# One encoder layer on one core: the second LayerNorm's scale taken block by block, its parameter rows in a ring slot, and the late branch moved into the 11th pair of experts

## The chip, the core and the metric

The kernel runs on one core of one Trainium2 chip. The metric is the device time of one execution in microseconds (us). Before the change it is 1922.2 us, the median of three runs (1920.51 to 1925.04).

## The reference, cut to what matters

One layer of an encoder over 256 tokens of width 2048. A mixer (not shown) gives y, and then:

```python
x = _layer_norm(ALPHA * x + y, ln1_g, ln1_b)
y = _hmoe(x, ...)      # 32 experts, each token goes to 2 of them
x = _layer_norm(ALPHA * x + y, ln2_g, ln2_b)

def run(args):         # one expert on its tokens
    e, idx, w = args
    xb = xf[idx]
    h = jax.nn.silu(xb @ w1[e]) * (xb @ w3[e])
    return (h @ w2[e]) * w[:, None]

def _layer_norm(x, g, b):
    mu = xf.mean(-1, keepdims=True)
    var = jnp.mean(jnp.square(xf - mu), -1, keepdims=True)
    return (xf - mu) * lax.rsqrt(var + LN_EPS) * g + b
```

w1 and w3 (gate and up) are 2048 x 512 per expert, w2 (down) is 512 x 2048, all float32: 12 MB for one expert and 384 MB for the 32.

## The kernel before, in words

The first 990 us or so compute the mixer, the first LayerNorm and the router. The rest, with which the change deals, is the expert phase and the second LayerNorm (LN2).

**Pairs.** The 32 experts are worked in 16 pairs (`for p in range(NP)`). Each expert has 64 places for tokens, so a pair fills the 128 rows. A pair does `gate_up` (16 steps of 4 products, `gu`; the trace shows each float32 product as two records), then `dispatch` of the next pair's tokens (`ps_d`), `turn_hidden` and `turn_places` (`pt_hs`, `pt_oh`), `down` (`py`, 32 products), and `combine` (`ps_c`), which adds the weighted rows into `acc`, the layer's sum of two halves of 128 tokens by 2048. The two last combines of a pair are kept in `pending` and run beside the next pair's first steps. `gate_up` takes a table `beside`, which says what other work is put ahead of which step.

**Loads.** A pair reads 24 MB in 24 loads of 1 MB: 8 of the gate matrices, 8 of the up matrices, 8 of the down matrices. Those of the last pair's down matrices go by the column blocks `LAST`. SP issues all of them in the order of the program (`loads_in_order`, a schedule by hand). `places()` hands out the buffer of each load: 18 slots of 1 MB in five rings (`RINGS`, taken in the order of `TURN`), tiles named `er`. A load waits until the last reader of its slot is done. It also waits for the load eight before it, because there are eight completion semaphores (DMAHW0 to DMAHW7), so at most eight are in flight. Semaphores DMASW are those of loads that POOL (GpSimd) issues.

**LayerNorm rows.** `ln1_g`, `ln1_b` and `ln2_g` lie as rows of 512 in `lnrow`, a part of `wrf` that belongs to the kernel for good. `ln_row(r)` spreads a row over the 128 partitions by a product with a column of the identity (`ps_ln`). `residual()`, in the pair with index 3 (the 4th), adds ALPHA times LN1's output to `acc`: eight calls beside steps 4 to 11 of that pair, each beginning with one `ln_row`. `ln2_scale()`, in the last pair, spreads `ln2_g` into one ring slot (four `ln_row` and four ScalarE copies), and loads `ln2_b` into another by one broadcast load of 1 MB.

**The end.** `down_last` does the last pair's down products by the blocks `LAST`; the combine of each block also takes the statistics (`bn_stats`) of the sum. Then come `ln2_stats()`, the branch `tc.If(most > CAP)` and the application of LN2 to eight pieces of 128 by 512. The branch handles experts with more than 64 tokens (`late_block`). It is not taken for these inputs. Six pieces are done by two VectorE passes each (L1316, L1317), two by ScalarE and two GpSimd passes, and each piece is stored when it is done.

The functions that the diff touches:

Of the kernel before, what the change touches and what calls it, by code (L numbers as in the profile page):

```python
# [19 lines left out]
P = 128  # L20
# [29 lines left out]
def kernel(ctx: ExitStack, tc: tile.TileContext, a, out):  # L50
# [173 lines left out]
    wr = glob.tile([P, KT, 36], F32, name="wr")  # L224
# [518 lines left out]
    def places():  # L743


        turn = [i for i in TURN for i in [i[0]] * i[1]]
        index = (i for i in count() if i not in (18, 19, 20))
        slot = lambda i: rings[i].tile([P, 2048], F32, tag="er", name="er")
        for i in turn:
            yield next(index), slot(i)  # L750
        yield 18, ys_p[0].tile([P, 2048], F32, tag="ys", name="er_ys")
        for s in range(2):
            yield 19 + s, x1p[0].tile([P, D], F32, tag=f"x1{s}", name="er_x1")
        while True:
            for i in turn:
                yield next(index), slot(i)

    place = places()

    def prefetch():  # L760
        i, t = next(place)
# [248 lines left out]
    lnrow = wrf[0:16, 0:512]  # L1010
    for j, k in enumerate(("ln1_g", "ln1_b", "ln2_g", "ln2_b")):
        nc.gpsimd.dma_start(lnrow[4 * j:4 * j + 4], a[k].rearrange("(m c) -> m c", c=512))

    def ln_row(r):

        pg = sm("ps_ln")
        PE.matmul(pg, ident[:16, r:r + 1].to_broadcast([16, P]), lnrow, start=True, stop=True)
        return pg

    gb2 = [], []  # L1020
    b2 = a["ln2_b"].rearrange("(o c) -> o c", o=1)

    def ln2_scale():
        while len(loads) - 1 not in loaded:
            prefetch()
        for b in gb2:
            b.append(next(place)[1])
        nc.sync.dma_start(gb2[1][0], b2.to_broadcast([P, D]))
        for c in range(4):
            S.activation(gb2[0][0][:, 512 * c:512 * (c + 1)], ln_row(8 + c), AF.Copy)  # L1030
            yield

    def residual():

        for c in range(4):
            cc = slice(512 * c, 512 * (c + 1))
            pg = ln_row(c)
# [7 lines left out]
            pg = ln_row(4 + c)  # L1045
# [10 lines left out]
    def late_block(e, b):  # L1056
# [3 lines left out]
        oh = ex_p[0].tile([P, 2, CAP], F32, tag="oh", name="oh_l", bufs=2)  # L1060
        ow = ex_p[0].tile([P, 2, CAP], F32, tag="ow", name="ow_l")
# [12 lines left out]
        for wv, o0 in ((w1v, 0), (w3v, 512)):  # L1074
            for k0 in range(0, KT, 2):
                wt = rings[2].tile([P, 1024], F32, tag="er", name="er_l")
                nc.sync.dma_start(wt, wv[ds(e, 1), :, k0 * DE:(k0 + 2) * DE].rearrange("e p f -> (e p) f"))
# [3 lines left out]
        hst = hs_p[0].tile([P, 2, DE], F32, tag="hs", name="hs_l")  # L1081
# [14 lines left out]
        for hf in range(2):  # L1096
            py = acc2("py_l")
            for k in range(4):
                wt = rings[2].tile([P, 1024], F32, tag="er", name="er_l")
                nc.sync.dma_start(wt, w2v[ds(e, 1), :, k, hf * 1024:(hf + 1) * 1024].rearrange("e p c -> (e p) c"))  # L1100
# [86 lines left out]

    def combine(c, ys, cb, w=512, first=False, last=False):
# [5 lines left out]
        for s in range(2):  # L1194
# [5 lines left out]
            if last:  # L1200
                V.bn_stats(stat[:, s, LAST.index((c, w))], o)

# [39 lines left out]

    acc = ys = None
    for p in range(NP):
# [3 lines left out]
        beside = {1: [finish], 2: [finish]} if p else {i: [lambda k=k: dispatch_part(0, k) for k in ks]  # L1248
# [3 lines left out]
        if p == RESIDUAL:  # L1252
            res = residual()
            beside |= {i: [lambda: next(res)] for i in range(4, 12)}
        if last:
            scale2 = ln2_scale()
            beside |= {i: [lambda: next(scale2)] for i in (10, 12, 14, 15)}
        hst = gate_up(p, beside)
        if last:
            S.activation(glob.tile([P, 1], F32, tag="warm", name="warm2"), hst[:, 0, 0:1], AF.Sqrt, bias=epsc, scale=0.0)  # L1260
            hT = turn_hidden(hst)
            cb, ws = turn_places(p)
            down_last(hT, cb, ws)
# [15 lines left out]
    products_in_order.close()  # L1279
    lmv = ex_p[0].tile([P, 2, 2], F32, name="lmv")  # L1280
# [3 lines left out]
    def ln2_stats():  # L1284
        for s in range(2):
            V.bn_aggr(lmv[:, s], stat[:, s])
        S.activation(lrs, lmv[:, :, 1], AF.Sqrt, bias=epsc)
        V.reciprocal(lrs, lrs)
        V.scalar_tensor_tensor(lnb, lmv[:, :, 0], -1.0, lrs, op0=OP.mult, op1=OP.mult)

    ln2_stats()
    loads_in_order.close()
    with tc.If(most > CAP):
        with tc.For_i(0, NE) as e:
            n = nc.values_load(cnt[0:1, ds(e, 1)], min_val=0, max_val=T)
            for b in range(1, T // CAP):
                with tc.If(n > b * CAP):
                    late_block(e, b)
        for s in range(2):
            for i, (c, w) in enumerate(LAST):  # L1300
                V.bn_stats(stat[:, s, i], acc[s][:, c:c + w])
        ln2_stats()


    ctx.enter_context(tc.manual_schedule(engines={mybir.EngineType.DVE, mybir.EngineType.Pool, mybir.EngineType.SP}))
    for i, pooled in ((0, 0), (1, 1), (2, 0), (5, 1), (3, 0), (4, 0), (7, 0), (6, 0)):
        s, c = divmod(i, 4)
        cc = slice(512 * c, 512 * (c + 1))
        g2, bb2 = (t[0][:, cc] for t in gb2)
        o = acc[s][:, cc]  # L1310
        if pooled:
            S.activation(o, o, AF.Identity, bias=lnb[:, s:s + 1], scale=lrs[:, s:s + 1])
            G.tensor_tensor(o, o, g2, op=OP.mult)
            G.tensor_tensor(o, o, bb2, op=OP.add)
        else:
            V.scalar_tensor_tensor(o, o, lmv[:, s, 0:1], g2, op0=OP.subtract, op1=OP.mult)  # L1316
            V.scalar_tensor_tensor(o, o, lrs[:, s:s + 1], bb2, op0=OP.mult, op1=OP.add)  # L1317
# [38 lines left out]
```

## Time and profile before

| what | value |
|---|---|
| median of three runs | 1922.2 us (1920.51 to 1925.04) |
| the profiled execution's own time | 1924.37 us |
| its span, first to last instruction | 1922.7 us |
| mean granted TensorE clock | 0.994 of full speed |
| busy: PE, DVE, ACT, POOL | 97%, 42%, 30%, 4% of the span |
| moved by DMA | 576.59 MB, mean 300 GB/s |

The profiled execution is 1.67 us longer than its span, and 2.2 us above the median of the runs. Busy shares are means over a dense first half, in which PE computes with the weights split in two parts, and the expert phase; the two have different limits and are to be read apart. PE is TensorE, DVE VectorE, ACT ScalarE, POOL GpSimd, and SP the engine that issues the weight loads. A q behind an engine's name means its instruction queue.

### The profile page before, as it was taken

What the parts mean: (1) busy time and instruction counts of PE and PEld (TensorE: products, weight loads), DVE (VectorE), ACT (ScalarE), POOL (GpSimd) and SP (SyncE); (2) the same over time, 40 slices, a digit from 0 to 9 for tenths busy, and PEclk for the clock granted to TensorE, in tenths of its full rate; (3) what the DMA queues carried; (4) which work ended last, traced back from release to release, by engine and by line L of the source; (5) the groups of instructions that cost most, each with busy time, mean ns of one, the idle gap of its engine ahead of it and who ended that gap; (6) DMA issues with size and microseconds to landing.
All of it is one profiled execution on the core that took longest, in us unless ns stands there. A gap on an engine that the chain in (4) does not pass through costs nothing. (4 is left out here: it accounts for less than half of the span.)

```text
span 1922.7 us, 28567 instructions
## 1 busy us (share of the span) xinstructions
PE 1865.2 (97%) x12006; PEld 1318.5 (69%) x12007; DVE 803.0 (42%) x1257; ACT 575.5 (30%) x807; POOL 74.4 (4%) x95
## 2 busy tenths in 40 slices
PE   9999999999999999999999999999999999999995
PEld 8989999999999999997753444444344443443432
DVE  6477685476545555555521234122122121221215
ACT  5464444466444444443430111011011010110111
POOL 3100001021000000000000000000000000000001
PEclk9999999999999999999999999999999999999997
DMA  9554565644555555679499999999999999999995
GB/s 276 179 171 143 156 195 176 186 143 137 177 186 187 187 186 187 229 257 356 140 420 396 419 419 420 419 419 420 419 419 420 419 420 419 419 420 420 420 414 200
DMA packets 148806, 576.59 MB, mean 300 GB/s; under 512 B 12348, under 2 KB 14784, under 8 KB 100416
## 3 DMA queue, kind: packets, MB, share of 16 engines
q1 hardware_dynamic: 146896, 571.52, 78.7%
q0 software_dynamic: 1776, 3.18, 0.6%
q8 instruction: 96, 1.57, 0.3%
q14 instruction: 38, 0.31, 0.0%
HBM read 572.54 MB, written 2.10 MB: 299 GB/s over the span
## 5 line engine op out<-in xcount | busy, mean ns | idle before, releaser
L177 PE MATMUL ps_t<-xh,whi 128*128 128x256 f32 x1856 | 522.7, 282 | 0.8 <-ACT xh L110 0.8
L177 PE MATMUL ps_t<-xl,whi 128*128 128x256 f32 x1856 | 521.4, 281 | 0.2 <-DVE xl L111 0.2
L177 PE MATMUL ps_t<-xh,wlo 128*128 128x256 f32 x1856 | 520.6, 280 | 0.0
L111 DVE TENSOR_TENSOR wlo<-wraw,whi 128x1024 fp32r<-128x1024 f32 (+1 forms) x313 | 385.6, 1234 | 322.1 <-ACT whi L110 321.7
L1147 PE MATMUL gu<-er,xe 128*64 128x512 f32 x2048 | 466.0, 596 | 27.4 <-DMA er<-in_w_exp_up_dram 27.4
L110 ACT ACTIVATE whi<-wraw 128x1024 fp32r<-128x1024 f32 (+1 forms) x313 | 330.3, 1057 | 437.6 <-PE ps_t L177 336.0
L1147 PEld LDWEIGHTS gu<-er,xe 128*64 128x64 f32 x2048 | 146.9, 137 | 318.8 <-issue 256.5
L177 PEld LDWEIGHTS ps_t<-xh,whi 128*128 128x128 f32 x1856 | 350.6, 189 | 2.0 <-ACT xh L110 1.1
L177 PEld LDWEIGHTS ps_t<-xl,whi 128*128 128x128 f32 x1856 | 350.7, 189 | 1.1 <-DVE xl L111 0.5
L177 PEld LDWEIGHTS ps_t<-xh,wlo 128*128 128x128 f32 x1856 | 350.0, 189 | 0.1
L1209 PE MATMUL py<-er,hs 128*64 128x512 f32 x936 | 206.4, 594 | 0.0
L1152 DVE TENSOR_TENSOR hs<-hs,gu 128x512 f32<-128x512 f32 x16 | 11.0, 688 | 406.1 <-ACT hs L1151 406.1
L1209 PEld LDWEIGHTS py<-er,hs 128*64 128x64 f32 x936 | 67.3, 137 | 125.2 <-issue 122.8
L1151 ACT ACTIVATE hs<-gu 128x512 f32<-128x512 f32 x16 | 9.6, 597 | 455.5 <-PE gu L1147 455.5
L1130 PEld LDWEIGHTS ps_d<-oh,xk 128*128 128x128 f32 x1024 | 118.0, 192 | 27.0 <-issue 24.3
L1185 DVE SCALAR_TENSOR_TENSOR ys<-py,ws,ys 128x512 fp32r<-128x512 f32 (+1 forms) x65 | 48.1, 740 | 190.8 <-ACT ys L1184 190.8
L1130 PE MATMUL ps_d<-oh,xk 128*128 128x128 f32 x1024 | 126.7, 279 | 0.9 <-DVE oh L1117 0.9
L1184 ACT ACTIVATE ys<-py,ws 128x512 fp32r<-128x512 f32 (+1 forms) x65 | 44.5, 684 | 250.5 <-PE py L1209 196.8
L1199 DVE TENSOR_TENSOR acc<-acc,ps_c 128x512 f32<-128x512 f32 (+1 forms) x122 | 77.4, 674 | 47.4 <-PE ps_c L1193 47.4
L1193 PE MATMUL ps_c<-ys,cb 128*128 128x512 f32 (+1 forms) x260 | 74.6, 417 | 0.8 <-DVE ys L1185 0.8
L1053 ACT ACTIVATE xe<-ps_d,b1k,g1k 128x128 f32<-128x128 f32 x128 | 48.2, 458 | 81.7 <-PE ps_d L1130 79.6
L177 PE MATMUL ps_t<-yh,whi 128*128 128x256 f32 x256 | 72.0, 281 | 0.0
(380 smaller groups left out, 1469.4 us busy)
## 6 DMA issues: line engine op xcount, KB each, us to landing
er<-in_w_exp_gate_dram SPq DMA_DIRECT2D x128, 1024.0 KB, 19.9
er<-in_w_exp_up_dram SPq DMA_DIRECT2D x128, 1024.0 KB, 19.9
er<-in_w_exp_down_dram SPq DMA_DIRECT2D x123, 1024.0 KB, 19.9
wraw<-in_w_gate_dram SPq DMA_DIRECT2D x128, 512.0 KB, 3.9
wraw<-in_w_in_dram SPq DMA_DIRECT2D x119, 512.0 KB, 3.9
wraw<-in_w_branch_dram SPq DMA_DIRECT2D x32, 512.0 KB, 3.7
wraw<-in_w_out_dram SPq DMA_DIRECT2D x32, 512.0 KB, 7.2
x<-in_x_dram POOLq DMA_DIRECT2D x8, 256.0 KB, 8.9
```

The lines of the kernel that those rows point to most:

```text
L110: S.activation(hi, src, AF.Copy)
L111: V.tensor_tensor(lo, src, hi.bitcast(F32), op=OP.subtract)
L177: PE.matmul(o, wt[:, k, m * P:(m + 1) * P], x[:, kk, :], start=(kk == 0 and i == 0 and (m % 2 == 0)), stop=(kk == nk - 1 and i == 2), skip ...
L1053: return S.activation(o, src, AF.Identity, bias=b1k[:, k:k + 1], scale=g1k[:, k:k + 1])
L1130: PE.matmul(pd[:, j * P:(j + 1) * P], xk[:, s, k + j], oh[:, s].rearrange("p e c -> p (e c)"), start=(s == 0), stop=(s == 1))
L1147: PE.matmul(gu[64 * j:64 * j + 64, o0:o0 + 512], xe[:, k, j], wt[j][:, k % 4 * DE:(k % 4 + 1) * DE], start=(k == 0), stop=(k == KT - 1))
L1152: V.tensor_tensor(hs, hs, gu[:, 512:1024], op=OP.mult)
L1184: S.activation(yh, src, AF.Copy, scale=ws)
L1185: V.scalar_tensor_tensor(yl, src, ws, yh.bitcast(F32), op0=OP.mult, op1=OP.subtract)
L1193: PE.matmul(pcs[s], cb[:, s * P:(s + 1) * P], ys[i], start=(i == 0), stop=(i == 1))
L1199: V.tensor_tensor(o, o, pcs[s], op=OP.add)
L1209: PE.matmul(py[c // 2][64 * j:64 * j + 64, c % 2 * 512:(c % 2 + 1) * 512], hT[:, k, 64 * j:64 * j + 64], wt[j][:, c * 512:(c + 1) * 512], ...
```

## The change

Four things are done.

1. The LayerNorm rows no longer have a place of their own. `load_rows()`, called at the beginning of the 4th pair, takes the next ring slot from `places()`. Eight POOL loads put `ln2_g` and `ln2_b` (three times each, interleaved) and the rows of LN1 into it. The LN2 rows are split into two parts whose sum is the row and kept in `rows2` for the end. `residual` reads its rows of LN1 out of the slot.
2. `ln2_g` is spread in the 15th pair, beside steps 4 to 8, into a ring slot taken then (`g2`) and held to the end. The broadcast load of `ln2_b` is gone.
3. After the statistics of a block of the last pair, `scale_last` multiplies that block of `acc` by `g2`. What is left of LN2 is `acc * rstd + (shift * ln2_g + ln2_b)`. The bracket for 128 tokens by 512 columns is one product of a 24-row matrix (`lhs`, made from the mean and the reciprocal deviation) with `rows2`, so one VectorE pass for each piece remains (L1357). GpSimd has no pass any more. Ahead of the last `turn_hidden` two products without use (`junk2`) are put.
4. The branch for late places runs ahead of the 11th pair (`late_places`, p == LATE + 2), after the combines that are pending. Inside it the loads go on ScalarE's queue.

```diff
+    def load_rows():
+        r = next(place)
+        rows, hi = r[0:24, 0:512], r[0:24, 512:1024]
+        for i in range(6):
+            nc.gpsimd.dma_start(rows.rearrange("(c i) x -> i c x", i=6)[i],
+                                a["ln2_b" if i % 2 else "ln2_g"].rearrange("(m c) -> m c", c=512))
+        for j, k in enumerate(("ln1_g", "ln1_b")):
+            nc.gpsimd.dma_start(r[24 + 4 * j:28 + 4 * j, 0:512], a[k].rearrange("(m c) -> m c", c=512))
...
+        S.activation(hi.bitcast(F32R), rows, AF.Copy)
+        rows2.append(glob.tile([24, 512], F32R, tag="wr", name="rows2"))
+        V.scalar_tensor_tensor(rows2[0], hi, sel, rows, op0=OP.mult, op1=OP.add)
+        return r[0:32, 0:512]
...
     def ln2_scale():
-        while len(loads) - 1 not in loaded:
-            prefetch()
-        for b in gb2:
-            b.append(next(place)[1])
-        nc.sync.dma_start(gb2[1][0], b2.to_broadcast([P, D]))
...
-            pg = ln_row(c)
+            pg = row(rows, 24 + c)
...
+    def scale_last(c, w):
+        for s in range(2):
+            o = acc[s][:, c:c + w]
+            V.tensor_tensor(o, o, g2[0][:, c:c + w], op=OP.mult)
...
+        if last and (c, w) != LAST[-1]:
+            scale_last(c, w)
...
+    def late_places():
+        while pending:
+            finish()
+        with tc.If(most > CAP):
...
+        if p == LATE + 2:
+            late_places()
...
         if p == RESIDUAL:
-            res = residual()
+            res = residual(load_rows())
             beside |= {i: [lambda: next(res)] for i in range(4, 12)}
-        if last:
+        if p == NP - 2:
+            g2.append(next(place))
+            nc.gpsimd.dma_start(g2[0][0:4, 0:512], a["ln2_g"].rearrange("(m c) -> m c", c=512))
             scale2 = ln2_scale()
-            beside |= {i: [lambda: next(scale2)] for i in (10, 12, 14, 15)}
+            beside |= {i: [lambda: next(scale2)] for i in range(4, 9)}
...
-    ln2_stats()
-    loads_in_order.close()
-    with tc.If(most > CAP):
...
+    for s in range(2):
+        V.bn_aggr(lmv[:, s], stat[:, s])
+    S.activation(lrs, lmv[:, :, 1], AF.Sqrt, bias=epsc)
+    scale_last(*LAST[-1])
+    V.reciprocal(lrs, lrs)
...
+    for i in range(8):
+        c, s = divmod(i, 2)
         cc = slice(512 * c, 512 * (c + 1))
-        g2, bb2 = (t[0][:, cc] for t in gb2)
+        pg = sm("ps_b")
+        PE.matmul(pg, lhs[:, c, s * P:(s + 1) * P], rows2[0], start=True, stop=True)
         o = acc[s][:, cc]
-        if pooled:
...
-            V.scalar_tensor_tensor(o, o, lmv[:, s, 0:1], g2, op0=OP.subtract, op1=OP.mult)
-            V.scalar_tensor_tensor(o, o, lrs[:, s:s + 1], bb2, op0=OP.mult, op1=OP.add)
+        V.scalar_tensor_tensor(o, o, lrs[:, s:s + 1], pg, op0=OP.mult, op1=OP.add)
         nc.sync.dma_start(out[s * P:(s + 1) * P, cc], o)
```

The first place is SP's queue, on the loads that run ahead while the pair with index 3 is computed: the last up load and the first four down loads of that pair. Before the change they stand there as follows (the number behind `er` is that of the tile, and the brackets hold the semaphores waited for):

```order
L763 DMA er_11564<-in_w_exp_up_dram 128x2048 [waits DMAHW1_49,PE_49]
L763 DMA er_11637<-in_w_exp_down_dram 128x2048 [waits DMAHW2_49,PE_49]
L763 DMA er_11639<-in_w_exp_down_dram 128x2048 [waits DMAHW3_49,PE_49]
L763 DMA er_11649<-in_w_exp_down_dram 128x2048 [waits DMAHW4_49,PE_49]
L763 DMA er_11651<-in_w_exp_down_dram 128x2048 [waits DMAHW5_49,PE_49]
```

The same five rows of the changed kernel:

```order
L763 DMA er_11577<-in_w_exp_up_dram 128x2048 [waits DMAHW1_49,PE_49]
L763 DMA er_11650<-in_w_exp_down_dram 128x2048 [waits DMAHW2_49,PE_49]
L763 DMA er_11652<-in_w_exp_down_dram 128x2048 [waits DMASW4_49,DMASW5_49,DMASW3_49,DMASW6_49,DMASW2_49,DMASW7_49,DMASW1_49,DMAHW3_49,DMASW0_49,PE_49]
L763 DMA er_11662<-in_w_exp_down_dram 128x2048 [waits DMAHW4_49]
L763 DMA er_11664<-in_w_exp_down_dram 128x2048 [waits DMAHW5_49]
```

The second down load now also waits for the eight POOL loads of the LayerNorm rows (DMASW), and its PE semaphore stands at another instruction: its slot is that of `er_11410`, the rows' tile. The two rows after it, and eight more that are not shown, wait only for the load eight before.

What PE does at that place in the changed kernel: the seventh and the eighth row product (`ps_ln`) of the residual among the gate and up products (`gu`) of steps 10 and 11 of the same pair.

```order
L1036 MATMUL ps_ln_11539<-er_11410,ident_125 128x512 [waits DVE_49,PE_49]
L1164 MATMUL gu_11426<-er_11547,xe_11267 64x512 [waits DMAHW4_49]
L1164 MATMUL gu_11426<-er_11549,xe_11267 64x512 [waits DMAHW5_49]
L1164 MATMUL gu_11426<-er_11547,xe_11267 64x512
L1164 MATMUL gu_11426<-er_11549,xe_11267 64x512
L1036 MATMUL ps_ln_11555<-er_11410,ident_125 128x512 [waits DVE_49]
L1164 MATMUL gu_11426<-er_11547,xe_11267 64x512
```

All row products read `er_11410`; the eighth one is its last reader, and it is the one for which the second down load waits. Before the change they read `wr`, and that load waited for a down product of the pair with index 2.

The third place is again SP's queue, between the last down loads of the 10th pair and the first gate loads of the 11th. Before:

```order
L763 DMA er_13253<-in_w_exp_down_dram 128x2048 [waits DMAHW0_49,PE_49]
L763 DMA er_13255<-in_w_exp_down_dram 128x2048 [waits DMAHW1_49,PE_49]
L763 DMA er_13303<-in_w_exp_gate_dram 128x2048 [waits DMAHW2_49,PE_49]
L763 DMA er_13305<-in_w_exp_gate_dram 128x2048 [waits DMAHW3_49,PE_49]
L763 DMA er_13331<-in_w_exp_gate_dram 128x2048 [waits DMAHW4_49,PE_49]
L763 DMA er_13333<-in_w_exp_gate_dram 128x2048 [waits DMAHW5_49,PE_49]
```

After (the rows left out are the branch's body, which is jumped over):

```order
L763 DMA er_13266<-in_w_exp_down_dram 128x2048 [waits DMAHW0_49,PE_49]
L763 DMA er_13268<-in_w_exp_down_dram 128x2048 [waits DMAHW1_49,PE_49]
L1270 COMPARE_AND_BRANCH
L1271 COMPARE_AND_BRANCH
L1271 UNCONDITIONAL_BRANCH [waits SP_sequencer_49,DMAHW0_49,DMAHW1_49,DMAHW2_49,DMAHW3_49,DMAHW4_49,DMAHW5_49,DMAHW6_49,DMAHW7_49]
...
L1270 UNCONDITIONAL_BRANCH [waits SP_sequencer_49,DMAHW0_49,DMAHW1_49,DMAHW2_49,DMAHW3_49,DMAHW4_49,DMAHW5_49,DMAHW6_49,DMAHW7_49]
L763 DMA er_13959<-in_w_exp_gate_dram 128x2048 [waits DMAHW2_49,PE_49]
L763 DMA er_13961<-in_w_exp_gate_dram 128x2048 [waits DMAHW3_49,PE_49]
```

Between the two loads there are now a compare and, where the branch is not taken, a block whose end waits for all eight load semaphores and for SP's own sequencer. Before the change the same block stood behind the last load of the program.

## Rows read from the trace of the kernel before

**Rows 1.** The page: 40 equal slices of the span, 48 us each

```profile
GB/s 276 179 171 143 156 195 176 186 143 137 177 186 187 187 186 187 229 257 356 140 420 396 419 419 420 419 419 420 419 419 420 419 420 419 419 420 420 420 414 200
```

**Rows 2.** Busy time by stretch: PE, PEld, DVE, ACT, POOL, clock, DMA share, GB/s

```profile
1200.00:1400.00 200.00, 200.00 (x1028) 89.04 (x1028) 44.44 (x89) 22.99 (x49) 0.00 (x0) 1.00 1.01 419
...
1600.00:1800.00 200.00, 188.01 (x929) 81.61 (x931) 42.57 (x84) 21.60 (x45) 0.00 (x0) 1.00 1.01 420
```

**Rows 3.** PE's timeline: start, length, line, operation, records, [idle before and its releaser]

```profile
1032.32 24.25 PE L1147 MATMUL gu<-er,xe 128*64 128x512 f32 x112
1087.03 24.25 PE L1147 MATMUL gu<-er,xe 128*64 128x512 f32 x112
...
1808.32 3.65 PE L1147 MATMUL gu<-er,xe 128*64 128x512 f32 x16 [1.33 <-DMA er<-in_w_exp_up_dram]
```

**Rows 4.** SP's timeline of issues, three stretches

```profile
1132.92 2.82 SPq L763 DMA_DIRECT2D er<-in_w_exp_down_dram  x2
...
1500.06 12.79 SPq L763 DMA_DIRECT2D er<-in_w_exp_down_dram  x6
...
1515.01 0.33 SPq L763 DMA_DIRECT2D er<-in_w_exp_gate_dram  x1
```

**Rows 5.** DMA issues of 1132 to 1134: KB each, us to landing

```profile
er<-in_w_exp_down_dram SPq DMA_DIRECT2D x1, 1024.0 KB, 19.9
```

**Rows 6.** PE's timeline in the pair with index 3

```profile
1135.77 1.94 PE L1147 MATMUL gu<-er,xe 128*64 128x512 f32 x8
...
1145.34 1.12 PE L1017 MATMUL ps_ln<-wr,ident 16*128 16x512 f32 x2
...
1165.77 1.12 PE L1017 MATMUL ps_ln<-wr,ident 16*128 16x512 f32 x2
```

**Rows 7.** SP's issue at 1031.29, and the DMA of 1031 to 1031.5

```profile
1031.29 0.80 SPq L763 DMA_DIRECT2D er<-in_w_exp_down_dram  x2
...
DMA packets 6, 0.02 MB, mean 49 GB/s; under 512 B 3, under 2 KB 3, under 8 KB 3
...
er<-in_w_exp_down_dram SPq DMA_DIRECT2D x1, 1024.0 KB, 4.8
```

**Rows 8.** PE's timeline behind the 10th pair's down products

```profile
1536.66 2.05 PE L1130 MATMUL ps_d<-oh,xk 128*128 128x128 f32 x16
1538.47 2.23 PE L1193 MATMUL ps_c<-ys,cb 128*128 128x512 f32 x8
...
1543.63 1.94 PE L1147 MATMUL gu<-er,xe 128*64 128x512 f32 x8
1545.50 1.20 PE L1193 MATMUL ps_c<-ys,cb 128*128 128x512 f32 x4
```

**Rows 9.** The branch's line: duration ns min/median/max, first and last start

```profile
L1293 SPq EVENT_SEMAPHORE  x9: 17/17/17, 1894.9 to 1898.8; - x9
...
L1293 SPq COMPARE_BRANCH  x1: 45/45/45, 1889.5 to 1889.5; - x1
L1293 PEldq COMPARE_BRANCH  x1: 3457/3457/3457, 1902.1 to 1902.1; - x1
```

**Rows 10.** The end, timeline of all engines

```profile
1895.05 0.69 DVE L1199 TENSOR_TENSOR acc<-acc,ps_c 128x512 f32<-128x512 f32 x1 [1.57 <-PE ps_c L1193]
...
1903.90 0.42 DVE L1286 BATCH_NORM_AGGREGATE lmv<-lstat 128x2 f32<-128x30 f32 x2
...
1904.68 0.17 DVE L1288 RECIPROCAL lrs<-lrs 128x2 f32<-128x2 f32 x1 [0.36 <-ACT lrs L1287]
...
1906.32 0.75 DVE L1316 SCALAR_TENSOR_TENSOR acc<-acc,lmv,er 128x512 f32<-128x512 f32 x1 [1.27 <-DVEq L1293]
...
1918.25 0.75 DVE L1317 SCALAR_TENSOR_TENSOR acc<-acc,lrs,er 128x512 f32<-128x512 f32 x1
```

**Rows 11.** Busy time of PE at the end: busy, clock, DMA share, GB/s

```profile
1880.00:1890.00 10.00, 9.87 (x42) 0.83 0.99 346
```

**Rows 12.** Groups of instructions on DVE and PE: busy us, mean ns, idle before

```profile
L1047 DVE SCALAR_TENSOR_TENSOR acc<-ps_ln,acc 128x512 f32<-128x512 f32 x8 | 5.1, 681 | 0.0
L1043 DVE TENSOR_TENSOR acc<-acc,ps_r 128x512 f32<-128x512 f32 x8 | 5.1, 677 | 0.0
...
L1017 PE MATMUL ps_ln<-wr,ident 16*128 16x512 f32 x24 | 13.4, 639 | 0.0
```

More of the change, by code (lines that the diff above doesn't have):

```diff
@@ L746, in places @@
         turn = [i for i in TURN for i in [i[0]] * i[1]]
-        index = (i for i in count() if i not in (18, 19, 20))
         slot = lambda i: rings[i].tile([P, 2048], F32, tag="er", name="er")
         for i in turn:
-            yield next(index), slot(i)
-        yield 18, ys_p[0].tile([P, 2048], F32, tag="ys", name="er_ys")
+            yield slot(i)
+        yield ys_p[0].tile([P, 2048], F32, tag="ys", name="er_ys")
         for s in range(2):
-            yield 19 + s, x1p[0].tile([P, D], F32, tag=f"x1{s}", name="er_x1")
+            yield x1p[0].tile([P, D], F32, tag=f"x1{s}", name="er_x1")
         while True:
             for i in turn:
-                yield next(index), slot(i)
+                yield slot(i)
     place = places()
+    issued = count()
     def prefetch():
-        i, t = next(place)
+        i, t = next(issued), next(place)
         src = loads[i]
@@ L1029, in ln2_scale, with residual @@
         for c in range(4):
[L1030 removed]
+            pgs.append(row(g2[0][0:4, 0:512], c))
             yield
[L1033 removed]
+        for c in range(4):
+            S.activation(g2[0][:, 512 * c:512 * (c + 1)], pgs[c], AF.Copy)
+        yield
+    def residual(rows):
         for c in range(4):
             cc = slice(512 * c, 512 * (c + 1))
[L1037 removed]
+            pg = row(rows, 24 + c)
             for s in range(2):
@@ L1044, in residual @@
             yield
-            pg = ln_row(4 + c)
+            pg = row(rows, 28 + c)
             for s in range(2):
@@ L1241, in finish @@
         combine(*pending.pop(0))
+    def late_places():
+        while pending:
+            finish()
+        with tc.If(most > CAP):
+            with tc.For_i(0, NE) as e:
+                n = nc.values_load(cnt[0:1, ds(e, 1)], min_val=0, max_val=T)
+                for b in range(1, T // CAP):
+                    with tc.If(n > b * CAP):
+                        late_block(e, b)
     acc = ys = None
@@ L1260 @@
             S.activation(glob.tile([P, 1], F32, tag="warm", name="warm2"), hst[:, 0, 0:1], AF.Sqrt, bias=epsc, scale=0.0)
-            hT = turn_hidden(hst)
             cb, ws = turn_places(p)
-            down_last(hT, cb, ws)
+            junk = sm("junk2")
+            xef = keep[p][0].rearrange("p k e c -> p (k e c)")
+            for i in range(2):
+                PE.matmul(junk, xef[:, 0:P], xef[:, 0:512], start=True, stop=True)
+            down_last(turn_hidden(hst), cb, ws)
             break
@@ L1308 @@
+    lhs = hs_p[0].tile([24, 4, 2 * P], F32R, tag="hs", name="lhs")
+    for c in range(4):
+        if c % 2:
+            S.activation(lhs[:, c], pt[:24, 0:2 * P], AF.Copy, scale=quarter[:, c:c + 1])
+        else:
+            V.tensor_scalar(lhs[:, c], pt[:24, 0:2 * P], quarter[:, c:c + 1], None, op0=OP.mult)
+    for i in range(8):
+        c, s = divmod(i, 2)
         cc = slice(512 * c, 512 * (c + 1))
-        g2, bb2 = (t[0][:, cc] for t in gb2)
+        pg = sm("ps_b")
+        PE.matmul(pg, lhs[:, c, s * P:(s + 1) * P], rows2[0], start=True, stop=True)
```

65 lines of the change are left out of this document (29 added, 36 removed).

## The prediction

> **What bounds the kernel now.** I read the page first: its slices of DMA rate show a first half at 140 to 260 GB/s and then, from slice 21 on (about 1010 us), 419 to 420 GB/s to slice 38 [rows 1]. The reader is to see one level without a dip for 850 us. Second, the busy time by stretch: at 1200 to 1400 PE is busy all 200 us and the DMA share is 1.01 too; at 1600 to 1800 PE falls to 188 while the DMA share stays [rows 2]. Third, PE's timeline for the reason: two early pairs start their long run of gate and up products 54.7 us apart (1032.32, 1087.03), and late in the kernel PE sits idle for up loads (1.33 us at 1808) [rows 3]. Fourth, SP's issues: five steps from 1500.06 take 12.79 - 0.33, so 2.49 us per load of 1 MB, and 24 x 2.49 = 59.8 us per pair [rows 4]. So the stream of loads needs 59.8 us per pair and PE less than that. PE starts behind the loads, with the ring full, eats into that stock and is starved from about the middle on. The stream is the bound from 1010 to the last load: a microsecond in which it stands still is a microsecond at the end. That is the question I put to each part.
>
> **The rows in a ring slot (part 1).** In the changed kernel the second down load of the pair with index 3 needs the slot of `er_11410`, and the last reader there is the eighth row product. In the trace of before these products lie in the gate and up steps of that pair, which begins at 1135.77: the first at 1145.34, the last from 1165.77 to 1166.89 [rows 6]. The load in question was issued at 1132.92 + 2.82 - 0.33 = 1135.41 [rows 4], and 19.9 us lie between issue and landing with eight in flight [rows 5], so it landed at 1155.3. Nothing that precedes it changes PE's place there, as the products are as many and at the same steps. So SP stops at 1135.4 and issues again at 1166.9. All loads sit behind it on SP's one queue, also the ten behind it that need no slot. Those in flight run out when the first down load lands, at 1132.92 + 19.9 = 1152.8. From an almost empty queue a load takes 4.8 us: the one of 1031.29, when the DMA moved 49 GB/s [rows 7]. So the second down load lands at 1166.9 + 4.8 = 1171.7 in place of 1155.3: **16.4 us** later, and with it all 300 or so behind it. The next loads go out at once, up to eight, so the rate is back at once but gives nothing back. The bounds: if the restart is 0.6 us quicker (the earlier load still had remnants before it) 15.8; if row products drift later by a microsecond, 17.4.
>
> A page of the Trainium skill speaks on this price: "SBUF — State Buffer", section "The DMA setup-cost knee", gives a transfer about 2 us plus its bytes over 436 GB/s, an estimate of 4.4 us for 1 MB where the row has 4.8. By it the stall would be 16.0, and the branch's 2.1. The row decides.
>
> **The branch in the 11th pair (part 4).** Not taken, the branch still has a block in which SP waits for all eight load semaphores. The trace of before shows that this block runs: nine semaphore events on SP from 1894.9 to 1898.8 behind a compare at 1889.5 [rows 9]. There the program had no load left to delay. Now it stands between the last down load of the 10th pair, issued 2.49 before 1515.01 [rows 4] and so landing at 1532.4, and the next gate load, which landed at 1534.9. After the change the gate load is issued when 1532.4 has passed, plus a tenth or two, and needs 4.8 [rows 7]: 1537.4, so **2.5 us** lost, again for good. The 5.4 us that SP took from the compare to its first event [rows 9] lie within the 19.9 us of draining, and cost nothing if they stay there. PE passes its own compare behind the pair's combines: these end at 1545.50 + 1.20 with two steps of 1.94 between them [rows 8] that now come later, so at 1542.8, and the compare takes 3.46 [rows 9]: about 1546.3, and VectorE's adds follow within a microsecond or so. The 10th and 12th loads after the branch wait for engines that are past it. Nine loads issued from 1532.6 land to 1537.4 + 8 x 2.49 = 1557.3, so the 10th keeps the queue fed if it is out by 1552: some 4 us to spare, hidden. With that cover gone it costs what is over. That the branch's body uses ScalarE's queue costs nothing, since it is jumped over. Bounds for this part: 2.3 (no tenths) to 2.5 + 5.4 = 7.9 (SP's fetch of its block begins only when the queue has drained).
>
> The slot for `g2` in the 15th pair leaves 17 slots. Two loads there then wait for a product on a load seven before them, which with 2.49 per load is 17 us after issue against 19.9 in flight; PE, starved, uses a load within a few us of its landing [rows 3]. I take nothing, with 3 us as upper bound. The row products and copies that leave the last pair lay beside starved PE; the broadcast lay behind all weight loads on the queue, and nothing but the old last passes waited for it. Nothing for either.
>
> **The end (parts 2 and 3).** Before: statistics done at 1903.90 + 0.42 = 1904.3, first pass at 1906.32 after 1.27 us of idle that the branch ends, last pass over at 1918.25 + 0.75 = 1919.0 [rows 10]: 14.7 us from statistics to last pass, and then 3.7 of storing to the span's end at 1922.7, which stays. After: DVE gets eight multiplications of 128x512 worth, 0.68 each by the nearest row [rows 12]. Two fit the 1.57 us for which DVE was idle before 1895.05 [rows 10]; a quarter (two halves) falls behind the statistics; four and two halves, 5 x 0.68 = 3.4, push the statistics back. Against it PE might run at full clock: granted 0.83 at 1880 to 1890 with 9.87 us busy [rows 11], worth up to 1.7 us if the two products without use keep it up. I take half, 0.9: statistics 2.5 later. From there ScalarE's root runs beside two half multiplications (0.7 in place of the 0.36 that DVE idled [rows 10]), reciprocal and shift 0.33, three short writes 0.6, two transposes and their handing over 0.7, `lhs` 0.5, first product 0.64 [rows 12] and its handing over: about 3.6 in place of 2.0 to the first pass. Eight passes from PSUM follow at 0.68 [rows 12]: 5.4 in place of 12.7. Sum after: 2.5 + 3.6 + 5.4 = 11.5 against 14.7, **3.2 us** gained. Bounds 1 (each handing over 0.3 longer, no clock) to 5 (DVE's multiplications at half price).
>
> **Sum.** 16.4 + 2.5 - 3.2 = +15.7. The profiled execution of before took 1924.37, so one like it would show about 1940.1; it lies 2.2 above the median, so the median forecast is 1922.2 + 15.7 = 1937.9.
>
> **Rivals.**
> *The hold costs nothing (no change).* If the pool gave the slot back when its copy is made, or the row products ran earlier, the stream would stay fed. It decides at 1152.8 - 4.8, about 1148: the last row product would have to end 19 us earlier, at the place of the second one. For it: the LN2 rows are copied out at once. Against it: LN1's rows are read from the slot by all eight products, and the order of the changed kernel shows the load waiting on PE. Then 1922.2 + 2.5 - 3.2 = 1921.5.
> *Faster: the stream has slack after all.* If PE and not the stream set the end, both stalls would vanish in stock that PE holds and the end's 3.2 would remain, 1919.0, or 1917 by its upper bound. It decides when the stock at the end is worth over 19 us. For it: PE is fully busy at 1200 to 1400. Against it: 12 us per 200 idle at 1600 to 1800 with the DMA share at 1.01 [rows 2].
> *The branch costs more.* SP's block is fetched after the drain, or DVE or ScalarE come past the branch too late for the 10th load; 5.4 more: 1943.3. The rows for it are PE's 3.46 us compare and SP's 5.4 [rows 9]; against it, SP's wait of nearly 20 us in which a fetch can end. The Trainium skill, "Runtime: NRT & Kernel Launch", section "Instruction fetch mechanics", says that a taken branch to a target outside the loaded window stalls for a fetch by DMA; the 3.46 us of PE agree with such a stall, and this rival is what it would do on SP.
>
> **How the numbers follow.** The forecast 0.76, the dearer branch 0.12, no change 0.07, faster 0.05. The forecast's own range is 15.8 + 2.3 - 5 = +13.1 to 17.4 + 2.5 + 3 - 1 = +21.9, 1935 to 1944; the dear branch lies inside. The range is drawn a little lower for an end that gains more and for runs that scatter by 2 us: 1932 to 1945, which leaves about 0.15 out. 0.2% is 3.8 us, about what the measurement can tell. Faster (below 1918.4): half of the last rival and a little for both mild cases, 0.05; same 0.07; slower 0.88.
>
> **What would show it.** In the changed profile SP shows a wait of about 31 us on a row product (`ps_ln`) near 1135, the DMA rate falls to nothing for about 16 us from 1153, and PE, which has stock there, starves earlier than before. Near 1550 (16 later than before) SP's wait at the branch's line ends with the last load in flight, and the DMA dips for 2 to 3 us. The second pass of LN2 is gone and the time from the last statistics to the last pass is about 9 us. The prediction is wrong if the rate has no hole at 1153, or if PE is busy to the end while loads wait for slots.

## The result, and the profile after

The changed kernel took 1941.14 us (median of 4 runs, 1940.60 to 1943.47) against 1922.14 (4 runs, 1920.51 to 1925.04): 1.010 times the time before, interval 1.0082 to 1.0117, so 19.0 us more (15.8 to 22.5 by the interval). The forecast was 1937.9 with a range of 1932 to 1945. The profiled execution took 1940.93 with a span of 1938.0, so the spans differ by 15.3. Of the 3.7 that lack to 19.0, 2.2 are those by which the profiled execution of before lay above its median, and 1.3 lie around the span.

The page's slices of DMA rate come first, as in [rows 1]; a slice is 48.5 us here.

```profile
GB/s 277 179 170 146 160 180 194 185 141 140 173 187 186 189 187 185 249 275 315 187 419 396 418 298 390 419 419 421 419 420 419 382 418 420 419 420 419 420 419 218
```

The level of 419 to 420 has two new dips: 298 and 390 in slices 24 and 25 (1114 to 1211 us), and 382 in slice 32 (1502 to 1550). SP's queue names what it waited for from 960 to 1940 (us in total, times, longest):

```profile
SPq L763 <- PE ps_ln L1036: 31.9, 2, 31.7
...
SPq L1270 <- SPq L1270: 19.5, 3, 16.8
SPq L763 <- DVEq L1270: 13.3, 1, 13.3
```

The three are 31.7 us for a row product, 19.5 at the branch's line, and 13.3 for VectorE to pass the branch. Before, the longest wait for a row product was 7.2 us, the branch's line had 8.7 in all and behind the last load, and SP waited for no engine to pass the branch. The time from issue to landing of single loads in the changed kernel (KB, us), issued in this order at 1130.65, 1164.80, 1526.84, 1547.29 and 1552.25:

```profile
er<-in_w_exp_down_dram SPq DMA_DIRECT2D x1, 1024.0 KB, 19.9
...
er<-in_w_exp_down_dram SPq DMA_DIRECT2D x1, 1024.0 KB, 4.8
...
er<-in_w_exp_down_dram SPq DMA_DIRECT2D x1, 1024.0 KB, 19.9
...
er<-in_w_exp_gate_dram SPq DMA_DIRECT2D x1, 1024.0 KB, 4.9
...
er<-in_w_exp_up_dram SPq DMA_DIRECT2D x1, 1024.0 KB, 21.4
```

The first pair is the hole: landings at 1150.5 and 1169.6, 19.1 apart in place of 2.49, so 16.6 lost. The second pair is the branch: 1546.7 and 1552.2, 5.5 apart, so 3.0 lost. What PE did at the hole and behind the branch (columns as in [rows 3]):

```profile
1163.65 1.12 PE L1036 MATMUL ps_ln<-er,ident 32*128 32x512 f32 x2
1164.70 8.80 PE L1164 MATMUL gu<-er,xe 128*64 128x512 f32 x40
...
1566.16 6.16 PE L1164 MATMUL gu<-er,xe 128*64 128x512 f32 x18 [6.54 <-DVEq L1270]
```

The eighth row product ends at 1164.77 and SP's held load leaves at 1164.80. PE itself has stock and stands still nowhere in the hole. Busy time by stretch shows both places (columns as in [rows 2]):

```profile
1150.00:1155.00 5.00, 5.00 (x20) 1.36 (x19) 4.38 (x6) 0.00 (x0) 0.00 (x0) 1.00 0.00 0
1155.00:1165.00 10.00, 10.00 (x34) 2.72 (x36) 7.49 (x11) 0.00 (x0) 0.00 (x0) 1.00 0.00 0
1165.00:1170.00 5.00, 5.00 (x26) 1.67 (x24) 1.27 (x3) 0.00 (x0) 0.00 (x0) 1.00 0.85 311
...
1542.00:1544.00 2.00, 2.00 (x12) 0.59 (x10) 0.00 (x0) 0.00 (x0) 0.00 (x0) 1.00 0.77 320
1544.00:1546.00 2.00, 2.00 (x12) 0.72 (x10) 0.00 (x0) 0.00 (x0) 0.00 (x0) 1.00 0.44 176
1546.00:1548.00 2.00, 2.00 (x12) 0.70 (x10) 0.00 (x0) 0.00 (x0) 0.00 (x0) 1.00 0.00 0
1548.00:1550.00 2.00, 2.00 (x12) 0.60 (x10) 0.00 (x0) 0.57 (x1) 0.00 (x0) 1.00 0.87 254
```

Two things are to be seen. In 1150 to 1165 PE is at 100% and the DMA moves nothing: nothing in PE's own numbers warns of the loss. And at the branch the rate falls before the last load has landed at 1546.7: 320 and 176 in the two stretches ahead of it. Against 420, the four stretches at the branch lack (100 + 244 + 420 + 166) / 420 x 2 = 4.4 us of transfer, not 3.0. The same count over the hole, in steps of 2 us from 1126 to 1226, gives 17.5.

The branch's line (duration in ns, first and last start), and the last work of DVE (as in [rows 9, 10]):

```profile
L1270 SPq EVENT_SEMAPHORE  x9: 17/17/17, 1527.4 to 1547.2; - x9
L1270 DVEq EVENT_SEMAPHORE  x2: 21/21/21, 1565.9 to 1566.0; - x2
...
L1270 PEldq COMPARE_BRANCH  x1: 6259/6259/6259, 1558.7 to 1558.7; - x1
```

```profile
1922.56 1.36 DVE L1208 TENSOR_TENSOR acc<-acc,er 128x512 f32<-128x512 f32 x3
1924.49 0.42 DVE L1334 BATCH_NORM_AGGREGATE lmv<-lstat 128x2 f32<-128x30 f32 x2
...
1928.45 5.33 DVE L1357 SCALAR_TENSOR_TENSOR acc<-acc,lrs,ps_b 128x512 f32<-128x512 f32 x8
```

From the statistics (1924.9) to the end of the last pass (1933.8) it is 8.9 us, before 14.7. Laid beside each other, the same load lands in the changed kernel 2.3 us earlier ahead of the hole, 14.3 later right behind it, 15.5 from the fourth load behind it on, 14.3 later again ahead of the branch, 17.3 right behind that, 18.8 from the eighth load behind it on, and 18.9 at the last (1895.1 and 1914.0). From there to the span's end it is 27.6 before and 24.0 after.

### The profile page after: what moved, and what is told of

Read it like the earlier page. It is cut to its first block, busy times and chain, and to the rows that moved or that the text cites. A ratio compares the mean times of both kernels' runs of the same rounds, so it can differ in the third digit from the quotient of the medians.

```text
span 1938.0 us, 28603 instructions
## 1 busy us (share of the span) xinstructions
PE 1874.5 (97%) x12020; PEld 1322.6 (68%) x12021; DVE 802.4 (41%) x1272; ACT 575.7 (30%) x808; POOL 71.2 (4%) x98
## 6 DMA issues: line engine op xcount, KB each, us to landing
er<-in_w_exp_gate_dram SPq DMA_DIRECT2D x128, 1024.0 KB, 19.9
er<-in_w_exp_up_dram SPq DMA_DIRECT2D x128, 1024.0 KB, 19.9
er<-in_w_exp_down_dram SPq DMA_DIRECT2D x123, 1024.0 KB, 19.9
```

## The experiments

My theory: the stream of loads sets the end; the slot lent to the rows stops it for some 16 us, the branch for 2.5 or more, and the new end gives 3 back. Rivals: PE, not the queue, pays for the row products; the branch costs what the engines' compares cost, not the drain; the end's gain comes from elsewhere than the new LN2. Of every kernel the median and the ratio to the kernel before, run beside it, are given; that kernel's medians were 1921.4 to 1922.0.

**LN1's rows in a tile of their own.** They leave the ring slot; the row product becomes four of 128 columns.

```diff
+        r1 = ex_p[0].tile([32, 128], F32, name="ln1_rows")
...
-            nc.gpsimd.dma_start(r[24 + 4 * j:28 + 4 * j, 0:512], a[k].rearrange("(m c) -> m c", c=512))
+            nc.gpsimd.dma_start(r1[16 * j:16 * j + 16], a[k].rearrange("(m c) -> m c", c=128))
...
-        return r[0:32, 0:512]
+        return r1
```

> The slot is given back when the LN2 rows are copied out, at the beginning of the 4th pair; the LN1 rows lie in a small tile of their own (32 rows of 128) and each row product becomes four of 128 columns. If the hold of the slot up to the last row product makes the hole of 16.6 us, the hole at 1150 is gone and the time is 1941.1 - 16.6 = 1924.5 (1923 to 1926). Rival: the loads stop there for another reason, or the stream loses the same time later in another place: then within 3 us of 1941.

1922.56 (11 runs, 1.0001, 0.9992 to 1.001): 18.6 less than the changed kernel, and 0.4 below the range expected. At the last landing, counted from the load ahead of the hole, it is 16.8 less. Its busy time in the place of the hole, and SP's wait for the slot:

```profile
1150.00:1175.00 25.00, 25.00 (x143) 12.87 (x142) 13.36 (x22) 0.60 (x1) 0.00 (x0) 1.00 1.01 420
```

```profile
SPq L763 <- DVE rows L1030: 5.4, 1, 5.4
```

The DMA has no gap. SP still waits for the slot, but 5.4 us with eight loads in flight cost nothing. The row products still run there, each in four pieces, so it was the hold and not their work.

**Row products four steps earlier**, in steps 0 to 7, the slot still lent.

```diff
-            beside |= {i: [lambda: next(res)] for i in range(4, 12)}
+            for i in range(8):
+                beside[i] = beside.get(i, []) + [lambda: next(res)]
```

> The residual's eight calls stand beside steps 0 to 7 in place of 4 to 11, nothing else is changed. The last row product then comes four steps of 1.87 us earlier, at about 1157 in place of 1164.7. If the hold is priced by its last reader, the hole shrinks by 7.5 us: 1933.6 (1932 to 1935). If a hole costs a fixed amount (a queue that is emptied and filled again), the time stays at 1941; if something other than the row products holds the load, it stays too.

1936.22 (5 runs, 1.0072, 1.0058 to 1.0086): 4.9 less, not 7.5. PE's timeline there:

```profile
1138.51 0.71 PE L1215 MATMUL ps_c<-ys,cb 128*128 128x512 f32 x2 [2.30 <-DVE ps_r L1058]
...
1161.00 1.12 PE L1036 MATMUL ps_ln<-er,ident 32*128 32x512 f32 x2
```

The residual's additions met the last pair's combines on DVE, PE waited for a buffer, and the last row product came not at 1157 but at 1162.1. By landings the hole shrank by 2.3 (14.3 for 16.6) while the product came 2.34 earlier measured from the last landing: microsecond for microsecond, as the theory has it; what I had wrong was how early the product can be. That the medians differ by 4.9 where the last landings differ by 2.5 (counted from the load ahead of the hole) seems to lie with the changed kernel's four runs: against the version with the own tile and the one without the branch, too, its median is 1.8 and 1.9 us higher than the landings make it. 0.9 us of that lies around the span (2.6 us in the median of its four runs, at most 2.0 in the other kernels); the rest is not explained.

**The changed kernel without the branch.** `late_places()` isn't called, so places beyond the first 64 of an expert are left out, and the two pending combines run beside the 11th pair's first steps as in other pairs.

> The changed kernel without the branch for late places, which is not taken for these inputs (the late places' work is left out). If the branch costs the draining of the load queue alone, 2.9 us come back: 1938.2. If the slower landings of the next loads (1.5 us more, while the engines wait at the branch) are its doing too, 4.4 come back: 1936.7. Rival: those 1.5 us are scatter of the stream, as it has elsewhere.

1936.13 (5 runs, 1.0073, 1.006 to 1.0087): 5.0 less. The stretch of the branch has no dip:

```profile
1545.00:1552.00 7.00, 7.00 (x41) 3.31 (x38) 1.50 (x2) 1.37 (x2) 0.00 (x0) 1.00 1.01 418
```

**Both: own tile, and no branch** (the late places left out here too).

> Both together, the rows copied out and no branch (late places' work left out): what the end alone is worth. If hold and branch are all that the change costs, and add up, 1941.1 - 16.6 - 4.4 = 1920.1, and by the end's gain of 3.6 us against the kernel before 1922.1 - 3.6 = 1918.5; so 1918 to 1921. Rival: the slot that is held for the spread row in the last two pairs, or the scaling by blocks, eats the end's gain: 1922 or more.

1919.84 (11 runs, 0.9989, 0.998 to 0.9998): 2.7 less than with the own tile and the branch. So the branch is worth 5.0 by the medians of one pair of kernels and 2.7 by those of the other. Counted on landings, from the load ahead of the branch on, the two pairs agree: 3.0 and 2.8 at the first load behind it, 4.5 and 4.7 at the twentieth, and 3.1 at the last load in both. The 1.5 us more come within nine loads behind the branch, in all five kernels with the branch in the 11th pair and all loads on SP, and at that place in none of the four without it. So they are the branch's and no scatter, though two of the three pairs of kernels (the third pair is the next two) win them back further on.

**The branch moved alone.** The kernel before with the branch in the 11th pair, its loads on ScalarE's queue, and the branch and second statistics at the end gone; LN2 is the old one.

```diff
+        if p == LATE + 2:
+            late_places()
...
-    with tc.If(most > CAP):
...
-        ln2_stats()
```

> The kernel before with one part of the change alone: the branch for late places ahead of the 11th pair (with its loads on ScalarE's queue and its small tiles in the hidden tile). The second statistics behind the branch go with it. If draining the load queue costs 2.9 us, and the slower landings behind it 1.5, and the end is freed of 1.3 us of waiting at the branch: 1922.0 + 4.4 - 1.3 = 1925.1 (1923.5 to 1926). Rival: the cost comes only together with the rows' slot or the spread row's slot: 1920.7.

1923.51 (12 runs, 1.0007, 0.9998 to 1.0015). The loss in the stream is there (5.4 us of transfer by the rate, and 4.8 at the last landing, counted from the load ahead of the branch against the kernel before). But from the last landing (1897.4) to the span's end (1921.4) it is 24.0, as in the changed kernel, though LN2 is the old one.

**The kernel before without any branch** (late places left out), to tell the end's two parts apart.

> The kernel before without its branch at the end (the late places' work left out). Shown so far: in the kernel before with the branch moved alone the stretch from the last weights' landing to the span's end fell from 27.6 to 24.0 us, which is what the changed kernel has. If the branch at the end costs 3.5 us there, and the new LN2 (scaling by blocks, product for the shift) adds nothing, this kernel takes 1921.9 - 3.5 = 1918.4, not more than the changed kernel with its rows copied out and no branch (1919.8). If the new LN2 is worth the 3 us that the prediction gave it, only the branch's wait of 1.3 us goes: 1920.6.

1919.92 (11 runs, 0.9995, 0.9986 to 1.0004): the same as own tile without branch, 1919.84, which has the new LN2. But it is only 1.4 less than the kernel before beside it (1921.36; by the interval from 2.7 less to 0.8 more), not 3.5. DVE's end in this run of the old LN2:

```profile
1901.81 0.42 DVE L1286 BATCH_NORM_AGGREGATE lmv<-lstat 128x2 f32<-128x30 f32 x2
1902.15 0.72 DVE L1306 SCALAR_TENSOR_TENSOR acc<-acc,lmv,er 128x512 f32<-128x512 f32 x1
...
1914.07 0.75 DVE L1307 SCALAR_TENSOR_TENSOR acc<-acc,lrs,er 128x512 f32<-128x512 f32 x1
```

The first pass now follows the statistics at once, where the branch had held it to 1906.32 [rows 10]. From the last landing (1894.4): statistics done after 7.8, the last pass 12.6 later, the span's end 3.3 after that. The changed kernel: 10.9, 8.9, 4.2. So the new LN2 saves 3.7 in its passes and pays 3.1 for the scaling ahead of the statistics and up to 0.9 in later stores (3.7 to 4.2 in the kernels with the new LN2, 3.3 to 3.7 with the old).

The profile of before has 9.2, 14.7 and 3.7 there, 3.9 more than this one. Of that 2.1 are the first pass's wait, 0.4 the stores, and 1.4 the later statistics, which the branch behind them does not explain. The first down products of the last pair, the same code in both, took (before, then this kernel):

```profile
1880.88 8.77 PE L1221 MATMUL py<-er,hs 128*64 128x512 f32 x32
1880.12 7.09 PE L1221 MATMUL py<-er,hs 128*64 128x512 f32 x32
```

The granted clock was 0.61 at 1880 to 1884 before and 1.00 here. In the two other profiles with the old LN2, both with the branch moved, the statistics are done 7.8 behind the last landing, as here. So 1.4 of the 3.9 can't be put down to the wait at the branch; which clock the other executions of the kernel before had is not known.

**The branch in the third pair**, with the own tile: there I took the ring to be full and PE ahead.

```diff
-        if p == LATE:
+        if p == 2:
             most = nc.values_load(cnt[0:1, NE:NE + 1], min_val=0, max_val=T)
...
-        if p == LATE + 2:
+        if p == 2:
             late_places()
```

> The rows copied out as before, and the branch ahead of the 3rd pair (index 2) in place of the 11th. PE still lags behind the loads there. If the drain is a fixed price wherever it stands in the stream, 2.9 us of the branch's cost remain: about the 1922.6 of the version with the branch in the 11th pair, or 1.5 less if the slower landings there came of the starved engines: 1921.1. If PE's stop at the branch (3.5 to 6.3 us) delays slots that the loads wait for at that time, more: 1925 or so.

1951.11 (5 runs, 1.0148): far off. SP's waits and the stretch:

```profile
SPq L763 <- DVEq L1278: 34.4, 1, 34.4
```

```profile
1060.00:1085.00 25.00, 22.13 (x110) 10.33 (x109) 9.98 (x20) 4.84 (x10) 0.00 (x0) 1.00 0.02 6
```

The fifth load behind the branch waits until DVE has passed it. SP, which runs far ahead, stood at its compare at 1039.4 and DVE came past at 1085.3. Landings stopped from 1061.1 to 1091.7, so this wait lost 28 us. It is the wait of 13.3 us in the changed kernel, there for the tenth load: nine loads landed to 1573.7, the tenth left at 1566.1 and would have landed alone by 1570.9, so 2.8 us were left of its cover.

**Four loads behind the branch on GpSimd's queue**, with the own tile, free to leave when they like.

```diff
-        nc.sync.dma_start(t if ...
+        (nc.gpsimd if 24 * (LATE + 2) <= i < 24 * (LATE + 2) + 4 else nc.sync).dma_start(t if ...
```

> The rows copied out, the branch in the 11th pair, and the first four loads behind it (the first four gate loads of the 11th pair) issued by GpSimd, which is long past its own branch. They wait for their slots alone, so the DMA queues have work while SP drains its own. If the branch's price is the empty queue, it is gone: 1922.6 - 3 to 4.4 = 1918 to 1919.8, as the version without a branch (1919.8), and faster than the kernel before by 0.1 to 0.2%. Rival: the price lies in the engines' stop, not in the queue: 1922.

1928.86 (5 runs, 1.0032, 1.002 to 1.0045): 6.3 slower than with all on SP. GpSimd issued them at 1494 to 1498, as soon as slots were free:

```profile
er<-in_w_exp_down_dram SPq DMA_DIRECT2D x5, 1024.0 KB, 28.6
er<-in_w_exp_gate_dram POOLq DMA_DIRECT2D x4, 1024.0 KB, 15.1
```

SP's loads then took 28.6 us in place of 19.9: from 1494 to 1512 the two queues together moved 420 GB/s, the rate that one has alone. The drain stood bare all the same, and with four loads fewer ahead of the load that waits for DVE (14.4 here) a second gap opened.

```profile
1538.00:1545.00 7.00, 7.00 (x37) 2.83 (x34) 1.17 (x2) 1.37 (x2) 0.00 (x0) 1.00 0.57 206
1556.00:1563.00 7.00, 5.59 (x14) 1.95 (x16) 0.00 (x0) 0.00 (x0) 0.00 (x0) 0.51 0.63 220
```

**The two products without use left out**, with the own tile.

> The rows copied out, without the two products without use ahead of the last down products. If they hold PE's granted clock up at the beginning of the last down products (1.00 where the kernel before had 0.83), the clock falls again, the products take up to 1.7 us longer, and the time rises by 0 to 1.7: 1922.6 to 1924.3. If the order of the two turns alone did it, or VectorE is the bound there, it stays at 1922.6.

1923.75 (11 runs, 1.0008, 0.9999 to 1.0016): 1.2 slower than with them, inconclusive; in its profile the granted clock is 0.74 and 0.83 at 1880 to 1888, but statistics come only 0.35 later from the last landing. Over all profiles, the clock stayed at 1.00 in the last pair's first down products in the nine kernels with the two products, and fell there in two of the five without them (before and this one). That speaks for them and does not show it.

**Loads on GpSimd held back by seven loads**, branch in the tenth pair, where the load that waits for DVE is the sixteenth.

```diff
+        after = 216 <= i < 220
+        if after:
+            G.tensor_copy(t[0:1, 0:1], every[i - 7][0:1, 0:1])
+        (nc.gpsimd if after else nc.sync).dma_start(t if ...
...
-        if p == LATE + 2:
+        if p == 9:
```

> The rows copied out; the branch ahead of the 10th pair (index 9) in place of the 11th, where the first load behind it that needs a slot of the branch's own ring is the 16th in place of the 10th; and the first four loads behind the branch issued by GpSimd, each held by a copy of one element until the load seven before it has landed, so that they are in flight while SP drains. If the price of the branch is the 2.9 us of an empty queue and 1.5 us of slower landings while the engines stand at the branch, the 2.9 go: 1922.6 - 2.9 = 1919.7 (1918.5 to 1921). If it is all the engines' stop, 1922.6.

1922.99 (11 runs, 1.0007). They shared the rate with SP's last loads and landed with them (1481.2 and 1481.0), so nothing was left for the drain:

```profile
1480.00:1487.00 7.00, 5.96 (x18) 2.04 (x19) 0.75 (x1) 1.38 (x2) 0.00 (x0) 0.65 0.65 238
```

**The same cover in the kernel with the branch moved alone.**

> The kernel before with the branch alone moved, ahead of the 10th pair, and the first four loads behind it issued by GpSimd, held in the same way. By the sum of what was measured: the branch moved alone, 1923.5, less the 2.9 us of the empty queue, 1920.6 (1919.5 to 1922). With the rows copied out it should stand beside the version with the new LN2 and the same cover, 1919.7; a clear difference between the two is the new LN2's.

1923.95 (11 runs, 1.0018, 1.0008 to 1.0028). Three of the four landed with SP's last load (1477.2 and 1477.0), as above. The fourth left GpSimd only at 1497.7, right after PE came past the branch (1497.2), so it covered nothing.

**All four held until the third load before the branch has landed.**

```diff
-            G.tensor_copy(t[0:1, 0:1], every[i - 7][0:1, 0:1])
+            G.tensor_copy(t[0:1, 0:1], every[213][0:1, 0:1])
```

> As the version with the rows copied out and the drain covered, with one difference: GpSimd's four loads are all held until the third load before the branch has landed. In that version they shared the DMA with SP's last loads and landed with them, at 1481.2 against 1481.0, so the queue was empty all the same. Held longer, two or more of them should still be in flight when SP is through: no gap of 5.4 us between two landings there, and 1923.0 - 2.9 = 1920.1 (1919 to 1921.5). If a gap of some 5 us stays, GpSimd's loads are still too early, and the time stays at 1923.

1918.97 (11 runs, 0.999, 0.9981 to 0.9999). The copies, the loads behind them, and the stretch of the drain:

```profile
1463.39 0.60 POOL L766 COPY er<-er 1x1 f32<-1x1 f32 x4 [366.29 <-DMA er<-in_w_exp_down_dram]
1464.33 2.14 POOL L767 DMA_DIRECT2D er<-in_w_exp_gate_dram  x4 [0.34 <-POOL er L766]
```

```profile
1464.00:1466.00 2.00, 2.00 (x12) 0.64 (x10) 0.00 (x0) 0.00 (x0) 1.67 (x4) 1.00 0.71 250
1465.00:1472.00 7.00, 7.00 (x36) 2.30 (x32) 0.35 (x1) 0.69 (x1) 1.47 (x3) 1.00 0.96 382
1472.00:1490.00 18.00, 10.59 (x44) 5.97 (x42) 7.60 (x12) 3.46 (x7) 0.00 (x0) 0.74 1.02 419
```

In steps of 2 us the lowest rate is 250, where the changed kernel had 176 and 0. The dip costs 1.5 us of transfer, counted as above, in place of 4.4, and of 5.2 in the version that released the loads too early and is 4.0 us slower. With nothing left out it is 22 us under the changed kernel and 0.1% under the kernel before, at the edge of the noise, and as fast as the versions with no branch.

## Why the prediction was right, point by point

- **The bound.** Right: PE is busy throughout the hole and every later load stays late to the end. PE starves earlier, as was said: its first wait of over 0.8 us for an up load is at 1275, before at 1440. One reading was off: slice 21 of [rows 1] begins at 961 us, not 1010, and slice 22 has 396, so the level without a dip begins with slice 23, at 1058.
- **The rows in the slot, 16.4.** Right: 16.6 from landing to landing, 17.5 by the rate, and 18.6 between medians when the hold is taken away. SP's wait was forecast as 31 us and is 31.7. The row for the restart held: 4.8 and 4.9. The Trainium skill ("SBUF — State Buffer", "The DMA setup-cost knee") would give an estimate of 4.4; the measurement decides.
- **The branch, 2.5.** The mechanism was right and the size off, in the step from "needs 4.8 [rows 7]" to 2.5 us lost. From landing to landing 3.0 were lost, as the next issue came 0.6 behind the last landing (1546.7 to 1547.3) and not a tenth or two. And I counted only from the last landing, where the queue moves less already ahead of it: by the rate it is 4.4 to 5.7 in three kernels where the branch stands so, by landings 4.5 to 4.8 nine loads on, by medians 2.7 to 5.0, and between the two profiles of before and after 4.6 on the last landing (14.3 to 18.9). The dearer branch as I told it, a fetch on SP behind the drain, did not occur: SP's compare and its first event at 1527.2 and 1527.4 lie in the drain. PE's compare took 6.26 us, not 3.46. That agrees with the stall for a fetch that the Trainium skill ("Runtime: NRT & Kernel Launch", "Instruction fetch mechanics") states for a taken branch to a target that is not loaded; that a fetch makes the 6.26 us is not shown here. DVE came past the branch 18.7 behind the first gate load's issue (1566.0 - 1547.3) where I had 13.7 (1546.3 - 1532.6) and a microsecond, so the wait behind it had 2.8 us of cover left, not 4. Where the cover is gone it cost 28 us (branch in the third pair).
- **`g2`'s slot and the moved rows, 0.** Right for the slot: the same loads land 18.8 us later than before ahead of the 15th pair's, throughout them and up to the last pair's up loads. For the moved rows no trace contradicts it.
- **The end, -3.2.** Between the two profiles -3.6, but for another reason, so that the two numbers agree is in part luck. The new passes were as short as forecast ("5.4 in place of 12.7", measured 5.33), but they are not the gain: the scaling ahead of them, the longer way to the first pass and the later stores pay it back, and without a branch at the end the old LN2 is as fast (1919.92 against 1919.84). The step that failed is to set the new LN2 against the 14.7 us of before, in which 2.0 are the first pass's wait for the branch, and that goes with part 4. Another 1.4 of the 3.6 are the slower down products in the profile of before (8.77 us in place of 7.09). The forecast had 0.9 for that clock and gave it to the two products without use; taking these out cost 1.2 by medians, within the noise. By medians the end is worth less: 1.4 when only the branch is taken out, and 2.2 with the new LN2 as well (1922.01 to 1919.84).
- **Sum.** On the landings 16.6 + 4.6 - 3.6 = 17.6, and with the 1.3 more around the span 18.9, where the medians differ by 19.0. The forecast's 15.7 lacks 2.1 for the branch and the 1.3 around the span, for which it had no term; the interval of the 19.0, 15.8 to 22.5, is wider than both. The two spans differ by only 15.3 since before's profiled execution was 2.3 late already ahead of the hole.

## What to carry to other kernels

A slot borrowed from the ring of a single in-order queue is paid not by its user but by every load behind it: put the time at which the last reader is done beside the time at which the queue would next want that slot, and copy small things out at once. A branch that is jumped over is not free where a queue runs at full rate, if its block, as here, makes the issuing engine wait for all its loads, and a load behind it may wait for the slowest engine to pass; look for a place with cover, and give the cover to a second queue only so late that it doesn't land with the first. When two edits end at the same place, take each out alone before naming the one that gained: here the old LN2 without the branch was as fast as the new one, so the end's gain came with the branch that left.

## What the runs showed of the hardware that was not expected

- A queue that runs empty loses more than the gap between landings: the rate went 426, 320, 176, 0, 254, 430 in steps of 2 us, 4.4 us of transfer for a gap of 3.0. The landings tell the same a little later: 3.0 late at the first load behind the branch and 4.5 at the eighth, 16.6 behind the hole and 17.8 from the fourth load on.
- Twelve loads of 1 MB land in 29.9 us nearly everywhere, and here and there in 31.4, at different places in kernels with the same code there, while the rate stays at 417 to 421. Where two kernels take such a step at different places, a difference between their landings grows or shrinks by 1.5 on the way, as the branch's 4.5 that was 3.1 at the last load. Their cause is open.
- A compare for a branch not taken took PE 3.46 us in the kernel before, 6.26 in the changed one and 6.37 with the own tile; the other engines' took under 0.1. In the third pair it was 3.39. What sets the length is not shown.
- The granted clock at the end differs between two executions whose code is the same up to there: a mean of 0.61 at 1880 to 1884 in the kernel before, between its two levels (1.2 and 2.4 GHz), and 1.00 without the branch, which stands behind that stretch. In both PE had been idle for 1.42 us just ahead (1878.0 to 1879.4, and 1877.3 to 1878.7).
